# The head of a convolutional FFN: when three half-matrix sums are formed, split and queued

## The chip, the cores and the metric

One core of one Trainium2 chip runs the whole program. The metric is the device time of one launch in microseconds (us); several launches of the same program give a median. TensorE (PE) does the matrix products, VectorE (DVE) and ScalarE (ACT) the element-wise work, GpSimd (POOL) a little of it, and SyncE (SP) issues the loads and stores.

## The reference

A decoder trunk of two layers over a stream of 1024 tokens by 1024 channels, all in float32. Each layer is a mixer and then an FFN; this is the part that matters here:

```python
def conv_glu_ffn(x, w_up, conv_w, conv_b, w_down):
    h = causal_depthwise_conv(x @ w_up, conv_w, conv_b)     # w_up: 1024 x 5632, 3 taps
    gate, val = jnp.split(h, 2, axis=-1)
    return (jax.nn.silu(gate) * val) @ w_down
...
        h = h + conv_glu_ffn(rmsnorm(h, ffn_norm[layer]), ffn_up[layer], ffn_conv_w[layer],
                             ffn_conv_b[layer], ffn_down[layer])
```

## The kernel before

Channels lie on the 128 partitions and tokens along the free dimension, in halves of 512 tokens. Every float32 operand of a product is split in two: a rounded high part (ScalarE copies it, L331) and a low part, the operand less its high part (VectorE, L332; `split`, L330). A product then is three matmuls per 128 channels: high by high, high by low, low by high. So each operand costs one ScalarE and one VectorE instruction before TensorE can use it.

An FFN layer (`ffn`, L526) goes over `f` = 0 to 21. A step `f` makes 128 gate channels `g` and 128 value channels `v` for all tokens. Step 0 is a plain projection (`proj_two`, L350; 96 matmuls of 128x512). After its first four input chunks it calls the hook `norms[1].rest` (L321), which finishes the norm of the second half of the tokens: eight chunks, each a scaling on VectorE (L317), a high copy on ScalarE and a low subtraction, on VectorE for even chunks and on GpSimd for odd ones (L319).

From step 1 on, the four half products of `g` and `v` are made out of seven products instead of eight, with sums of halves of the input and of the weights (a Strassen form). With y11, y21, y12, y22 the four quarters of the normed input `hT` (channels 0 to 511 or 512 to 1023 of the first or second 512 tokens), the input sums are T1 = y12 - y11, T2 = y22 - T1, T3 = y22 - y12 and T4 = y21 - T2. `tokens` (L624) forms them in place in `hT` and splits them: T1 into the second half of `AH`/`AL`, T2, T3, T4 into `TH`/`TL`. The products of a step stand in the loop of L661 in this order, 12 matmuls of 128x512 each: `11` and `21` (with weights `a`), `2` (`b`), `1` (`d`), `3` (`c`), `22` (`b`), `4` (`c`), into the PSUM tiles `X` and `YZ`. The weights of step `f` + 1 are prepared during step `f` by `prep_a` (the split of the gate weights), `prep_s` (sums), `prep_b`, `prep_c` and `prep_d` (splits); each frees a load buffer `wst`, and the load of the next weights waits for that. The `Tail` of a step (convolution taps at L607, silu, product, store) runs during the next step. The tail of step 0 reads its `g` and `v` straight out of PSUM (`0g`, `0v`), where two tiles of this size fit.

A scheduler puts the instructions of each engine in one order, which the engine keeps: an instruction that waits holds all behind it on its engine. So the place of an instruction in its engine's order says what it waits behind.

There are two FFN layers, so the head of the FFN comes twice, at about 355 to 417 us and 1519 to 1578 us of the span. The hook `norms[1].rest` is also called at the head of the odd layer's mixer, at about 1040 to 1060 us.

Of the kernel before, what the change touches and what calls it, by code (L numbers as in the profile page):

```python
# [24 lines left out]
NF = DFF // P  # L25
# [110 lines left out]
def trunk(ctx: ExitStack, tc: tile.TileContext, x, mix0_norm, mix0_w_in, lru_conv_w, lru_conv_b,  # L136
# [149 lines left out]
    class Norm:  # L286
# [24 lines left out]
            dve.scalar_tensor_tensor(r0, q, 1.5, r0, op0=ALU.add, op1=ALU.mult)  # L311
            self.r = r0

        def chunk(self, c):
            s = HALF[self.h]
            y = self.hT[:, c, s] if self.put else t2(f"y_{self.name}{c}")
            dve.scalar_tensor_tensor(y, self.hT[:, c, s], self.gcol(c), self.r,  # L317
                                     op0=ALU.mult, op1=ALU.mult)
            split(AH[:, c, s], AL[:, c, s], y, pool if c % 2 else dve)  # L319

        def rest(self):  # L321
            self.rstd()
            for c in range(DC):
                self.chunk(c)

    def rsqrt_set():

        act.activation(junk, eps, AF.Abs_reciprocal_sqrt)

    def split(h, l, src, eng=None):  # L330
        act.copy(h, src)  # L331
        (eng or dve).tensor_tensor(l, src, h.bitcast(F32), op=ALU.subtract)  # L332

    def proj_half(ps, w, s, hook=None):
        wh, wl = w
# [190 lines left out]
    def ffn(ly, norms):  # L526
# [39 lines left out]
        def prep_b(f):  # L566
            w = ws[f]
            w["b"] = W.pair()
            split(*w["b"], w["g"])
            W.done()  # L570
# [50 lines left out]
                dve.tensor_tensor(self.cv, self.cv, self.cg, op=ALU.mult)  # L621
                nc.sync.dma_start(hid[ly][:, self.f], self.cv)

        def tokens():  # L624

            hT = st["hT"]
            y11, y21, y12, y22 = (hT[:, a, s] for s in HALF for a in (slice(0, 4), slice(4, 8)))
            for k in (slice(0, 2), slice(2, 4)):
                dve.tensor_tensor(y11[:, k], y12[:, k], y11[:, k], op=ALU.subtract)  # L629
                dve.tensor_tensor(y12[:, k], y22[:, k], y12[:, k], op=ALU.subtract)  # L630
                dve.tensor_tensor(y22[:, k], y22[:, k], y11[:, k], op=ALU.subtract)
                split(TH[:, 0, k], TL[:, 0, k], y22[:, k])
            split(*Y["1"], y11)
            split(*Y["3"], y12)
            dve.tensor_tensor(y21, y21, y22, op=ALU.subtract)  # L635
            split(*Y["4"], y21)


        prev = Tail(0, *proj_two(f"{ly}g0", f"{ly}v0", norms[1].rest))
        prep_a(1)  # L640
        prep_s(1, 0)
        prep_s(1, 1)
        tokens()
        prep_b(1)
        prep_d(1)
        prep_c(1)
        prev.ident()
        close_h()
        w2_cm = tc.tile_pool(name=f"w2{ly}", bufs=1)
        W.more = w2[0] = w2_cm.__enter__()  # L650
        slots = [(AH[:, c], AL[:, c]) for c in range(DC)]
        th6, tl6 = (t.rearrange("p a b t -> p (a b t)").rearrange("p (s t) -> p s t", t=T)
                    for t in (TH, TL))
# [5 lines left out]
            split(*slots[slot], r)  # L659

        for f in range(1, NF):  # L661
            w, nxt = ws.pop(f), f + 1 if f + 1 < NF else None
# [11 lines left out]
            prev.silu()  # L674
            dve.tensor_tensor(g[:, HALF[0]], y_, p1, op=ALU.add)
            prev.conv_v(1)
            prod(X, w["b"], 0, "2", False)
            u2 = t2(f"u2{ly}{f}")
            act.copy(u2, X)
            prev.conv_v(0)  # L680
            prev.end()
            prod(z_, w["d"], 0, "1")
            p5 = t2(f"p5{ly}{f}")
            act.copy(p5, z_)
            if nxt:
# [20 lines left out]
            prev.ident()  # L706
        W.ahead(2)
        for c in range(4, 8):
            stage(c, c)
        prev.conv_g()  # L710
        prev.silu()
        prev.conv_v(1)
        prev.conv_v(0)
        prev.end()
        W.more = w2[0] = None
        w2_cm.__exit__(None, None, None)
        fd_cm.__exit__(None, None, None)
# [663 lines left out]
```

## Time and profile before

| what | us |
|---|---|
| median of 3 runs | 2218.29 |
| lowest and highest of them | 2216.78, 2218.61 |
| the profiled execution, its own time | 2214.68 |
| its span in the trace | 2212.9 |
| TensorE busy | 2146.9 (97%) |
| VectorE busy | 1456.2 (66%) |
| ScalarE busy | 1011.1 (46%) |
| GpSimd busy | 114.3 (5%) |

Busy shares are means over a program whose stages differ. TensorE idles 66 us in all of the span; a wait in a stage where TensorE is the busiest engine lengthens the program, if nothing later takes the time up again. The views used below are the sums by stretch (windows), the waits of an engine, and the timeline of an engine, all of the one profiled execution.

### The profile page before, as it was taken

Reading aid. Unit: us, or ns where it says so; the run is one execution under the profiler, and the core shown is the slowest. Engines: PE = TensorE matmul, PEld = TensorE weight load, DVE = VectorE, ACT = ScalarE, POOL = GpSimd, SP = SyncE. Lnnn points to the kernel's source line nnn. Section 1 sums busy time; section 2 is a strip of 40 time slices with the busy share of each in tenths; the row PEclk is TensorE's granted clock in tenths of the full one; section 3 lists DMA queues with packets and bytes.
Section 4 is the critical chain, followed back from the end, with each engine's and each line's share of the span. In section 5 each row is a group of like instructions: output and inputs, shape, how many; then the busy total and the mean of one; then the engine's idle time right before and its main releaser. Section 6 shows DMA issues by size and latency. Waiting matters only on the chain. (4 is left out here: it accounts for less than half of the span.)

```text
span 2212.9 us, 25475 instructions
## 1 busy us (share of the span) xinstructions
PE 2146.9 (97%) x9789; PEld 1757.7 (79%) x9789; DVE 1456.2 (66%) x2046; ACT 1011.1 (46%) x1389; POOL 114.3 (5%) x141
## 2 busy tenths in 40 slices
PE   7999999899999999999899999899899999999998
PEld 6888887788888888887678887687688888888887
DVE  7555658977777773347476667768987777773344
ACT  6333544455555551124466575644555555551113
POOL 1000001000000000004211111001000000000000
PEclk9999999899999999999999999999999999999999
DMA  5111442222222272234222211552222222282212
GB/s 160 38 48 48 126 136 72 92 80 86 86 86 86 86 275 80 83 124 124 62 61 57 80 54 50 166 167 76 93 79 86 86 86 86 86 285 84 74 53 76
DMA packets 264353, 213.76 MB, mean 97 GB/s; under 512 B 8464, under 2 KB 233680, under 8 KB 264232
## 3 DMA queue, kind: packets, MB, share of 16 engines
q1 hardware_dynamic: 264040, 211.85, 30.8%
q8 instruction: 77, 1.26, 0.2%
q0 software_dynamic: 192, 0.30, 0.1%
q14 instruction: 44, 0.36, 0.1%
HBM read 165.94 MB, written 44.07 MB: 95 GB/s over the span
## 5 line engine op out<-in xcount | busy, mean ns | idle before, releaser
L108 ACT CAST wh<-wst 128x1024 fp32r<-128x1024 f32 (+2 forms) x134 | 134.1, 1001 | 514.9 <-PE dp L731 284.3
L109 DVE TENSOR_TENSOR wl<-wst,wh 128x1024 fp32r<-128x1024 f32 (+2 forms) x126 | 146.4, 1162 | 102.1 <-ACT wh L108 101.9
L733 DVE TENSOR_TENSOR hT_f<-dp,hT_f 128x512 f32<-128x512 f32 x96 | 65.9, 690 | 223.5 <-PE dp L731 221.9
L731 PE MATMUL dp<-AH,wh 128*128 128x512 f32 x432 | 168.1, 391 | 0.3 <-DVE hT_f L733 0.3
L731 PE MATMUL dp<-AH,wl 128*128 128x512 f32 x432 | 168.0, 389 | 0.0
L731 PE MATMUL dp<-AL,wh 128*128 128x512 f32 x432 | 167.9, 390 | 0.0
L587 PE MATMUL X<-TH,wl 128*128 128x512 f32 x312 | 124.1, 398 | 8.9 <-DVE wl L332 8.9
L587 PE MATMUL X<-TH,wh 128*128 128x512 f32 x312 | 123.9, 397 | 6.3 <-ACT p L669 5.7
L587 PE MATMUL X<-TL,wh 128*128 128x512 f32 x312 | 123.6, 396 | 0.0
L331 ACT CAST wh<-wst 128x1024 fp32r<-128x1024 f32 x78 | 80.9, 1054 | 64.5 <-PE YZ L587 45.8
L607 DVE SCALAR_TENSOR_TENSOR cg<-g,par_c,cg 128x1023 f32<-128x1023 f32 x84 | 107.5, 1280 | 1.8 <-ACT cg L601 1.6
L607 DVE SCALAR_TENSOR_TENSOR cv<-v,par_c,cv 128x1023 f32<-128x1023 f32 x84 | 107.2, 1276 | 0.1
L338 PE MATMUL op<-AH,wh 128*128 128x512 f32 x256 | 101.9, 398 | 1.9 <-DVE yt L1191 1.3
L338 PE MATMUL op<-AH,wl 128*128 128x512 f32 x256 | 100.5, 392 | 0.0
L338 PE MATMUL op<-AL,wh 128*128 128x512 f32 x256 | 100.4, 392 | 0.0
L332 DVE TENSOR_TENSOR wl<-wst,wh 128x1024 fp32r<-128x1024 f32 x78 | 95.2, 1222 | 7.2 <-ACT wh L331 7.1
L731 PEld LDWEIGHTS dp<-AH,wh 128*128 128x128 f32 x432 | 81.1, 188 | 18.4 <-DVE hT_f L733 0.7
L731 PEld LDWEIGHTS dp<-AL,wh 128*128 128x128 f32 x432 | 81.1, 188 | 17.5 <-DVE AL L332 0.4
L731 PEld LDWEIGHTS dp<-AH,wl 128*128 128x128 f32 x432 | 81.1, 188 | 16.9
L587 PE MATMUL YZ<-AH,wh 128*128 128x512 f32 x208 | 81.2, 390 | 0.0
L587 PE MATMUL YZ<-AL,wh 128*128 128x512 f32 x208 | 81.0, 389 | 0.0
L587 PE MATMUL YZ<-AH,wl 128*128 128x512 f32 x208 | 80.9, 389 | 0.0
(424 smaller groups left out, 5762.3 us busy)
## 6 DMA issues: line engine op xcount, KB each, us to landing
wst<-in_ffn_up_dram SPq DMA_DIRECT2D x88, 512.0 KB
hid<-cv SPq DMA_DIRECT2D x44, 512.0 KB
hr<-hid SPq DMA_DIRECT2D x44, 512.0 KB
wst<-in_mix_w_in_dram SPq DMA_DIRECT2D x40, 512.0 KB
wst<-in_ffn_down_dram SPq DMA_DIRECT2D x35, 512.0 KB
wst<-in_mix_w_out_dram SPq DMA_DIRECT2D x32, 512.0 KB
hdr<-hT_o SPq DMA_DIRECT2D x32, 256.0 KB
hT_f<-hdr SPq DMA_DIRECT2D x16, 512.0 KB
```

The costliest lines, as they stand in the source:

```text
L108: self.nc.scalar.copy(wh[:, :k, :m], w[:, :k, :m])
L109: (eng or self.eng).tensor_tensor(wl[:, :k, :m], w[:, :k, :m], wh[:, :k, :m].bitcast(F32), op=ALU.subtract)
L331: act.copy(h, src)
L332: (eng or dve).tensor_tensor(l, src, h.bitcast(F32), op=ALU.subtract)
L338: pe.matmul(ps, a[:, k], b[:, k, s], start=(k == 0 and i == 0), stop=(k == DC - 1 and i == 2))
L587: pe.matmul(ps, a[:, k0 + k], b[:, k], start=(first and k == 0 and i == 0), stop=(k == 3 and i == 2), skip_group_check=True)
L607: dve.scalar_tensor_tensor(dst[:, dl:], src[:, :T - dl], taps[j](c), dst[:, dl:], op0=ALU.mult, op1=ALU.add)
L731: pe.matmul(ps, p_[:, k], q_[:, s], start=(k == 0 and i == 0), stop=(k == n - 1 and i == 2))
L733: dve.tensor_tensor(hT[:, oc, s], ps, hT[:, oc, s], op=ALU.add)
```

## The change

`norms[1].rest` puts all eight low subtractions on VectorE. This holds for both FFN heads and for the mixer's head.

In the FFN head, `tokens` is taken apart. T1 and T2 come first, T1 in place by one instruction and T2 in two halves into scratch tiles of its own (two of the ring `t4`); T2 is split at once, then come the weights `b` and `d` of step 1. The result of step 0 is copied out of PSUM into two `t4` tiles, so its tail reads SBUF. What is left of `tokens` is called in step 1 behind ScalarE's copy `p1` of the first product: T1's split and half of T3 stand behind T2's splits, the rest of T3, the weights `c`, T4 and the copy of `0v` stand behind `p1` in ScalarE's order and behind T1's split in VectorE's (`tc.issue_after` adds an order on the same engine, and no wait across engines). T3 and T4 are split in halves. The whole tail of step 0 goes to the end of step 1. A small edit leaves the list of weights in place (`ws[f]` for `ws.pop(f)`).

```diff
-    def chunk(self, c):
+    def chunk(self, c, eng=None):
...
-            split(AH[:, c, s], AL[:, c, s], y, pool if c % 2 else dve)
+            split(AH[:, c, s], AL[:, c, s], y, eng or (pool if c % 2 else dve))
     def rest(self):
         self.rstd()
         for c in range(DC):
-            self.chunk(c)
+            self.chunk(c, dve)
...
-        def tokens():
-            hT = st["hT"]
-            y11, y21, y12, y22 = (hT[:, a, s] for s in HALF for a in (slice(0, 4), slice(4, 8)))
-            for k in (slice(0, 2), slice(2, 4)):
-                dve.tensor_tensor(y11[:, k], y12[:, k], y11[:, k], op=ALU.subtract)
-                dve.tensor_tensor(y12[:, k], y22[:, k], y12[:, k], op=ALU.subtract)
-                dve.tensor_tensor(y22[:, k], y22[:, k], y11[:, k], op=ALU.subtract)
-                split(TH[:, 0, k], TL[:, 0, k], y22[:, k])
-            split(*Y["1"], y11)
-            split(*Y["3"], y12)
-            dve.tensor_tensor(y21, y21, y22, op=ALU.subtract)
-            split(*Y["4"], y21)
-        prev = Tail(0, *proj_two(f"{ly}g0", f"{ly}v0", norms[1].rest))
+        p0 = proj_two(f"{ly}g0", f"{ly}v0", norms[1].rest)
         prep_a(1)
         prep_s(1, 0)
         prep_s(1, 1)
-        tokens()
+        y11, y21, y12, y22 = (st["hT"][:, a, s] for s in HALF
+                              for a in (slice(0, 4), slice(4, 8)))
+        tt2 = [t4(f"T2{i}{ly}").rearrange("p (k t) -> p k t", k=2) for i in range(2)]
+        ks = slice(0, 2), slice(2, 4)
+        dve.tensor_tensor(y11, y12, y11, op=ALU.subtract)
+        for k, t in zip(ks, tt2):
+            dve.tensor_tensor(t, y22[:, k], y11[:, k], op=ALU.subtract)
+            t2h, t2l = split(TH[:, 0, k], TL[:, 0, k], t)
         prep_b(1)
+        first = [t4(f"{n}0{ly}") for n in "gv"]
+        act.copy(first[0], p0[0])
         prep_d(1)
-        prep_c(1)
-        prev.ident()
-        close_h()
...
+        def tokens(p1):
+            with tc.issue_after(t2h.ins), tc.issue_after(t2l.ins):
+                _, t1l = split(*Y["1"], y11)
+                dve.tensor_tensor(y12[:, ks[0]], y22[:, ks[0]], y12[:, ks[0]], op=ALU.subtract)
+            with tc.issue_after(p1.ins), tc.issue_after(t1l.ins):
+                dve.tensor_tensor(y12[:, ks[1]], y22[:, ks[1]], y12[:, ks[1]], op=ALU.subtract)
+                split(TH[:, 1, ks[0]], TL[:, 1, ks[0]], y12[:, ks[0]])
+                prep_c(1)
+                split(TH[:, 1, ks[1]], TL[:, 1, ks[1]], y12[:, ks[1]])
+                act.copy(first[1], p0[1])
+                for k, t in zip(ks, tt2):
+                    dve.tensor_tensor(y21[:, k], y21[:, k], t, op=ALU.subtract)
+                    split(TH[:, 2, k], TL[:, 2, k], y21[:, k])
+            close_h()
...
+        prev = Tail(0, *first)
...
             prod(X, w["a"], 0, "11")
             p1 = t2(f"p1{ly}{f}")
-            act.copy(p1, X)
+            late = f == 1
+            c1 = act.copy(p1, X)
+            if late:
+                w2_cm = tokens(c1)
...
-            prev.conv_g()
+            if not late:
+                prev.conv_g()
...
             if nxt:
                 prep_c(nxt)
+            if late:
+                prev.whole()
             prev = Tail(f, g, v)
             prev.ident()
```

In the rows of the orders below the number behind a name tells buffers apart, and lines from L331 down to L332 keep their numbers in both kernels.

**The end of the norm on VectorE, first FFN head.** `hT_o` <- `r_no` is the scaling of a chunk, `AL` its low subtraction, `wst` the last weight sum of step 1. Before:

```order
L317 SCALAR_TENSOR_TENSOR hT_o_1722<-hT_o_1722,par_a,r_no_2497 128x512 x3
L332 TENSOR_TENSOR AL<-hT_o_1722,AH 128x512
L317 SCALAR_TENSOR_TENSOR hT_o_1722<-hT_o_1722,par_a,r_no_2497 128x512
L332 TENSOR_TENSOR AL<-hT_o_1722,AH 128x512
L317 SCALAR_TENSOR_TENSOR hT_o_1722<-hT_o_1722,par_a,r_no_2497 128x512 x3
L332 TENSOR_TENSOR AL<-hT_o_1722,AH 128x512
L317 SCALAR_TENSOR_TENSOR hT_o_1722<-hT_o_1722,par_a,r_no_2497 128x512
L332 TENSOR_TENSOR AL<-hT_o_1722,AH 128x512
```

Now:

```order
L317 SCALAR_TENSOR_TENSOR hT_o_1722<-hT_o_1722,par_a,r_no_2497 128x512 x3
L332 TENSOR_TENSOR AL<-hT_o_1722,AH 128x512 x3
L317 SCALAR_TENSOR_TENSOR hT_o_1722<-hT_o_1722,par_a,r_no_2497 128x512 x3
L332 TENSOR_TENSOR AL<-hT_o_1722,AH 128x512 x3
L317 SCALAR_TENSOR_TENSOR hT_o_1722<-hT_o_1722,par_a,r_no_2497 128x512 x2
L564 TENSOR_TENSOR wst_2395<-wst_2395 128x512
L332 TENSOR_TENSOR AL<-hT_o_1722,AH 128x512 x2
```

The four subtractions of the odd chunks, which stood on GpSimd, have joined the four of the even ones here.

**The sums and splits on VectorE, right behind.** L629 to L635 (now L645 to L666) are the sums, `TL` the low parts of T2, T3, T4, `AL` of 128x4x512 that of T1, `wl` and `dl` those of the weights of step 1 (`wst_2395`: `b`; `wst_2434`: `c`). Before:

```order
L564 TENSOR_TENSOR wst_2395<-wst_2395 128x512
L629 TENSOR_TENSOR hT_o_1722<-hT_o_1722 128x2x512 x2
L630 TENSOR_TENSOR hT_o_1722<-hT_o_1722 128x2x512 x2
L631 TENSOR_TENSOR hT_o_1722<-hT_o_1722 128x2x512 x2
L332 TENSOR_TENSOR AL<-hT_o_1722,AH 128x4x512
L332 TENSOR_TENSOR TL_2477<-hT_o_1722,TH_2476 128x1024 x2
L332 TENSOR_TENSOR TL_2477<-hT_o_1722,TH_2476 128x2048
L635 TENSOR_TENSOR hT_o_1722<-hT_o_1722 128x4x512
L332 TENSOR_TENSOR wl_2638<-wst_2395,wh_2637 128x1024
L332 TENSOR_TENSOR dl_2644<-s_2615,dh_2643 128x512
L332 TENSOR_TENSOR wl_2648<-wst_2434,wh_2647 128x1024
L332 TENSOR_TENSOR TL_2477<-hT_o_1722,TH_2476 128x2048
```

Now:

```order
L645 TENSOR_TENSOR hT_o_1722<-hT_o_1722 128x4x512
L332 TENSOR_TENSOR wl_2630<-wst_2395,wh_2629 128x1024
L647 TENSOR_TENSOR T_2620<-hT_o_1722 128x1024
L647 TENSOR_TENSOR T_2621<-hT_o_1722 128x1024
L332 TENSOR_TENSOR dl_2639<-s_2615,dh_2638 128x512
L332 TENSOR_TENSOR TL_2477<-T_2620,TH_2476 128x1024
L332 TENSOR_TENSOR TL_2477<-T_2621,TH_2476 128x1024
L658 TENSOR_TENSOR hT_o_1722<-hT_o_1722 128x2x512
L332 TENSOR_TENSOR AL<-hT_o_1722,AH 128x4x512
L660 TENSOR_TENSOR hT_o_1722<-hT_o_1722 128x2x512
L332 TENSOR_TENSOR TL_2477<-hT_o_1722,TH_2476 128x1024
L332 TENSOR_TENSOR wl_2667<-wst_2434,wh_2666 128x1024
```

The low part of the weights `b` (`wl_2638`) stood behind eleven sums and splits and now (`wl_2630`) stands behind one sum; T2 (`T_2620`, `T_2621`) is split next, and T1, T3 and the weights `c` (`wl_2667`) follow. Behind the last row stand now: the second half of T3's split, the two sums of T4, the low part of step 2's weights `a` (`wl_2688`), T4's two splits, and only then `g` of step 1.

**The copies on ScalarE in the same stretch.** `wh` are high parts of weights, `p` the copy of the first product, `cg` and `cv` the start of step 0's tail. Before:

```order
L331 CAST wh_2637<-wst_2395 128x1024
L601 ACTIVATE cg_2653<-0g_2481,par_c_1730 128x1024
L331 CAST AH<-hT_o_1722 128x4x512
L331 CAST TH_2476<-hT_o_1722 128x2048
L331 CAST TH_2476<-hT_o_1722 128x1024 x2
L331 CAST wh_2647<-wst_2434 128x1024
L602 ACTIVATE cv_2654<-0v_2482,par_c_1730 128x1024
L669 COPY p_2677<-X_2661 128x512
L331 CAST TH_2476<-hT_o_1722 128x2048
```

Now:

```order
L331 CAST wh_2629<-wst_2395 128x1024
L651 COPY g_2635<-0g_2481 128x1024
L331 CAST TH_2476<-T_2620 128x1024
L331 CAST TH_2476<-T_2621 128x1024
L693 COPY p_2658<-X_2642 128x512
L331 CAST AH<-hT_o_1722 128x4x512
L331 CAST wh_2666<-wst_2434 128x1024
L331 CAST TH_2476<-hT_o_1722 128x1024
L664 COPY v_2636<-0v_2482 128x1024
L331 CAST wh_2687<-wst_2633 128x1024
L331 CAST TH_2476<-hT_o_1722 128x1024
L708 COPY u_2716<-X_2642 128x512
```

The copy `p` (now L693) has moved from behind T1, T2, T3 and the weights `c` to right behind T2; `0g` and `0v` are copied instead of read by the tail. TensorE's order moves with it: the product `21` of step 1 (into `YZ`) stood behind `2` and `3` in the first head, and now stands right behind `11`, ahead of `2`; in the first head four matmuls of step 2's weights `a` now stand between `2` and `3`.

## Rows read from the trace of the kernel before

**Rows 1.** Windows: start:end, length, busy per engine (instructions), granted clock, DMA.

```profile
381.70:417.33 35.63, 26.93 (x98) 20.21 (x96) 32.85 (x29) 18.80 (x20) 0.00 (x0) 0.81 0.26 80
1545.52:1578.40 32.88, 25.10 (x97) 19.25 (x96) 31.09 (x28) 16.41 (x18) 0.00 (x0) 0.84 0.26 80
354.69:381.70 27.01, 24.42 (x99) 17.86 (x98) 24.60 (x28) 12.52 (x16) 6.62 (x4) 1.00 0.03 11
1518.51:1545.52 27.01, 24.44 (x100) 17.86 (x98) 24.60 (x28) 12.52 (x16) 6.63 (x4) 1.00 0.03 11
420.00:780.00 360.00, 360.00 (x1590) 298.16 (x1590) 278.17 (x304) 188.49 (x228) 0.00 (x0) 1.00 0.28 85
```

**Rows 2.** Waits of TensorE, first FFN head: waiter <- releaser: us, times, longest.

```profile
PE X L587 <- DVE wl L332: 4.4, 1, 4.4
PE X L587 <- ACT p L669: 2.8, 1, 2.8
PE 0g L338 <- POOL AL L332: 1.8, 3, 0.8
PE 0g L338 <- DVE AL L332: 0.8, 2, 0.6
PE YZ L587 <- DVE g L675: 0.8, 1, 0.8
PE X L587 <- ACT u L679: 0.7, 1, 0.7
```

**Rows 3.** Timeline: start, length, engine, line, work; TensorE after the second wait.

```profile
393.26 0.63 PE L587 MATMUL X<-TH,wh 128*128 128x512 f32 x1
393.68 0.63 PE L587 MATMUL X<-TL,wh 128*128 128x512 f32 x1
```

**Rows 4.** Timeline, VectorE, first FFN head (merged rows: first start to last end).

```profile
363.24 2.07 DVE L317 SCALAR_TENSOR_TENSOR hT_o<-hT_o,par_a,r_no 128x512 f32<-128x512 f32 x3
365.23 0.68 DVE L332 TENSOR_TENSOR AL<-hT_o,AH 128x512 fp32r<-128x512 f32 x1
365.83 1.77 DVE L317 SCALAR_TENSOR_TENSOR hT_o<-hT_o,par_a,r_no 128x512 f32<-128x512 f32 x1
...
377.98 2.35 DVE L630 TENSOR_TENSOR hT_o<-hT_o 128x1024 f32<-128x1024 f32 x2
380.25 2.35 DVE L631 TENSOR_TENSOR hT_o<-hT_o 128x1024 f32<-128x1024 f32 x2
382.52 2.28 DVE L332 TENSOR_TENSOR AL<-hT_o,AH 128x2048 fp32r<-128x2048 f32 x1
384.73 4.55 DVE L332 TENSOR_TENSOR TL<-hT_o,TH 128x1024 fp32r<-128x1024 f32 x3
...
391.40 1.21 DVE L332 TENSOR_TENSOR wl<-wst,wh 128x1024 fp32r<-128x1024 f32 x1
...
396.48 1.27 DVE L607 SCALAR_TENSOR_TENSOR cg<-0g,par_c,cg 128x1023 f32<-128x1023 f32 x1
```

**Rows 5.** Timeline, GpSimd, the same head.

```profile
365.38 1.67 POOL L332 TENSOR_TENSOR AL<-hT_o,AH 128x512 fp32r<-128x512 f32 x1 [28.06 <-ACT AH L331]
```

**Rows 6.** Waits of TensorE, second FFN head (the row on p is as above).

```profile
PE X L587 <- DVE wl L332: 4.5, 1, 4.5
...
PE X L587 <- ACT wh2x L331: 0.4, 1, 0.4
```

**Rows 7.** Timeline, TensorE, head of the odd layer's mixer.

```profile
1060.12 0.60 PE L996 MATMUL 1q<-AH,wh 128*128 128x512 f32 x1 [3.85 <-DVE qs L1065]
```

**Rows 8.** Windows, the same place.

```profile
1060.31:1063.72 3.41, 3.41 (x9) 2.66 (x9) 0.92 (x2) 1.26 (x3) 0.76 (x2) 0.50 0.37 82
```

**Rows 9.** Timeline, SyncE's queue and ScalarE: a weight load and who waits for it.

```profile
407.27 8.43 SPq L87 DMA_DIRECT2D wst<-in_ffn_up_dram  x2
...
410.90 1.05 ACT L331 CAST wh2x<-wst 128x1024 fp32r<-128x1024 f32 x1 [0.29 <-DMA wst<-in_ffn_up_dram]
```

More of the change, by code (lines that the diff above doesn't have):

```diff
@@ L330, in split @@
     def split(h, l, src, eng=None):
-        act.copy(h, src)
-        (eng or dve).tensor_tensor(l, src, h.bitcast(F32), op=ALU.subtract)
+        return (act.copy(h, src),
+                (eng or dve).tensor_tensor(l, src, h.bitcast(F32), op=ALU.subtract))
     def proj_half(ps, w, s, hook=None):
@@ L622, in end, with rest, whole @@
                 nc.sync.dma_start(hid[ly][:, self.f], self.cv)
-        def tokens():
-            hT = st["hT"]
-            y11, y21, y12, y22 = (hT[:, a, s] for s in HALF for a in (slice(0, 4), slice(4, 8)))
-            for k in (slice(0, 2), slice(2, 4)):
-                dve.tensor_tensor(y11[:, k], y12[:, k], y11[:, k], op=ALU.subtract)
-                dve.tensor_tensor(y12[:, k], y22[:, k], y12[:, k], op=ALU.subtract)
-                dve.tensor_tensor(y22[:, k], y22[:, k], y11[:, k], op=ALU.subtract)
-                split(TH[:, 0, k], TL[:, 0, k], y22[:, k])
-            split(*Y["1"], y11)
-            split(*Y["3"], y12)
-            dve.tensor_tensor(y21, y21, y22, op=ALU.subtract)
-            split(*Y["4"], y21)
-        prev = Tail(0, *proj_two(f"{ly}g0", f"{ly}v0", norms[1].rest))
+            def rest(self):
+                self.conv_g()
+                self.silu()
+                self.conv_v(1)
+                self.conv_v(0)
+                self.end()
+            def whole(self):
+                self.ident()
+                self.rest()
+        p0 = proj_two(f"{ly}g0", f"{ly}v0", norms[1].rest)
         prep_a(1)
@@ L642, in ffn @@
         prep_s(1, 1)
-        tokens()
+        y11, y21, y12, y22 = (st["hT"][:, a, s] for s in HALF
[6 more added lines that the diff above has]
+            t2h, t2l = split(TH[:, 0, k], TL[:, 0, k], t)
         prep_b(1)
+        first = [t4(f"{n}0{ly}") for n in "gv"]
+        act.copy(first[0], p0[0])
         prep_d(1)
-        prep_c(1)
-        prev.ident()
-        close_h()
-        w2_cm = tc.tile_pool(name=f"w2{ly}", bufs=1)
-        W.more = w2[0] = w2_cm.__enter__()
+        def tokens(p1):
[12 more added lines that the diff above has]
+            close_h()
+            w2_cm = tc.tile_pool(name=f"w2{ly}", bufs=1)
+            W.more = w2[0] = w2_cm.__enter__()
+            return w2_cm
+        prev = Tail(0, *first)
         slots = [(AH[:, c], AL[:, c]) for c in range(DC)]
@@ L661, in ffn @@
         for f in range(1, NF):
-            w, nxt = ws.pop(f), f + 1 if f + 1 < NF else None
+            w, nxt = ws[f], f + 1 if f + 1 < NF else None
             X = psml(f"X{ly}{f}")
@@ L668, in ffn @@
             p1 = t2(f"p1{ly}{f}")
-            act.copy(p1, X)
+            late = f == 1
+            c1 = act.copy(p1, X)
+            if late:
+                w2_cm = tokens(c1)
             if nxt:
                 prep_a(nxt)
-            prev.conv_g()
+            if not late:
+                prev.conv_g()
             prod(y_, w["a"], 4, "21")
-            prev.silu()
+            if not late:
+                prev.silu()
             dve.tensor_tensor(g[:, HALF[0]], y_, p1, op=ALU.add)
-            prev.conv_v(1)
+            if not late:
+                prev.conv_v(1)
             prod(X, w["b"], 0, "2", False)
@@ L679, in ffn @@
             act.copy(u2, X)
-            prev.conv_v(0)
-            prev.end()
+            if not late:
+                prev.conv_v(0)
+                prev.end()
             prod(z_, w["d"], 0, "1")
@@ L709, in ffn @@
             stage(c, c)
[L710 to L714, printed above, removed]
+        prev.rest()
         W.more = w2[0] = None
```

## The prediction

> **What bounds the kernel now.** First read the windows [rows 1]. The last row is the bulk of an FFN: 360 us in which TensorE never idles, 1590 matmuls, 0.2264 us each (0.2267 with the few missing records), a product of 12 in 2.72 us. There nothing is to be had from the order of the other engines. The first two rows are the stretches this change is about: from the first product of step 1 to the first matmul of product `21` of step 2, each with exactly 96 matmuls of the same size. At the full pace they take 96 x 0.2267 = 21.8 us; they took 35.6 and 32.9. The excess is 13.9 us in the first FFN and 11.1 us in the second. The next two rows are the norms ahead of them, also 96 big matmuls each plus two small float32 ones of some 1.1 us together: 27.0 us each, 4.1 more than 22.9.
>
> Second, the waits say what ends this idle time [rows 2, 6]. In the first stretch TensorE waits 2.8 us until its own bank `X` is copied (ACT `p`), 4.4 us for the low part of the weights `b` (DVE `wl`), and twice 0.7 to 0.8; in the second 4.5 and 0.4, and the same 2.8 for `p`. In the norm it waits five times for the low part of a chunk, 2.6 us in all, 1.8 of it for GpSimd; the second norm repeats this (its busy time is the same to 0.02 us [rows 1]).
>
> Third, the clock. In the first stretch the granted clock is 0.81 in the mean [rows 1]: after the two long waits matmuls start 0.42 to 0.43 us apart, the pace of the 1.2 GHz level [rows 3]. A mean of 0.81 over 35.6 us is 35.6 x 0.19 / 0.5 = 13.5 us at that level; in the second stretch 32.9 x 0.16 / 0.5 = 10.5 us. So the 13.9 us are 8.7 us of waits, 0.1 us of slower first matmul behind each, and the rest, near 4.8 us, the low clock.
>
> Fourth, VectorE. It is busy 32.9 of 35.6 us there and 24.6 of 27.0 in the norm [rows 1], and the wait of 4.4 us ends with the row at 391.40, `wl` [rows 4]: eleven sums and splits for products 1, 2, 3 and 4 stood ahead of it. So it is a matter of order on VectorE.
>
> **The change, part by part.** Start-to-start costs on VectorE come from [rows 4]: 0.67 us for a scaling (three from 363.24 to 365.23), 0.60 for a 512 subtraction (365.23 to 365.83), 1.14 for a 1024 one (377.98 to 380.25 for two), 2.21 for a 2048 one (382.52 to 384.73).
>
> *Norm.* Four low subtractions go from GpSimd to VectorE. The row at 365.83 is a scaling that took 1.77 us where its kind takes 0.74 (2.07 for three that overlap); it lies under GpSimd's 1.67 us subtraction of 365.38 to 367.05 [rows 5]. So each of the four GpSimd rows holds up a VectorE row by about 1.0 us, and a subtraction on VectorE costs 0.60: 4 x 0.60 - 4 x 1.0 = 1.6 us less on VectorE, not 2.4 more. The Trainium skill, Perfetto Trace Analysis (Optimizing Scalar/DVE Operations), says that a saturated VectorE may gain from work given to another engine, "or even GPSIMD", with the warning that the two share a read port. By its first half this edit would cost 2.4 us a norm; the row above is on the side of the warning.
>
> Walk VectorE's new order from 363.24, where nothing ahead has changed: 3 scalings to 365.2, 3 subtractions to 367.0, 3 and 3 again to 370.8, 2 scalings and a weight sum to 372.8, the last 2 subtractions to 374.0. The last low part is there at 374.0, where GpSimd's was at 375.9 (the last of the five waits). The chunks come in threes, which leaves about one wait of 0.2 us by the same walk. TensorE starts step 1 some 2.9 us earlier (2.6 of waits and 5 x 0.1, less that one): at 378.8 instead of 381.7.
>
> *Sums.* Walk on: T1 (one row of 2.21) to 376.2, `wl` of `b` to 377.3, T2 to 379.6, `dl` to 380.2, T2's low parts to 382.5, half of T3 to 383.6, T1's low part to 385.8, half of T3 to 387.0, its low part to 388.1, `wl` of `c` to 389.2, the other low part to 390.4, T4 to 392.7, `wl` of step 2's `a` to 393.8, T4's low parts to 396.1, then `g`. ScalarE's copies keep ahead: it was busy 18.8 of 35.6 us [rows 1], and the added copies of `0g` and `0v` are two instructions of 128x1024, about 1.1 us each by the cast at 410.90 [rows 9]. Queuing behind `p` holds nothing up that VectorE could have taken: `p` ends near 382, when VectorE is still at T2.
>
> TensorE: product `11` from 378.8, `21` from 381.5, `2` from 384.2. What `2` needs is there at 382.6 (T2) and 378.5 (`wl`): the waits of 2.8 and 4.4 us are gone, partly since `21` now stands ahead of `2` as 2.72 us of cover, partly since `wl` comes 14 us sooner. `2` ends at 386.9. Then four matmuls of step 2, 0.9 us, and product `3`, which needs `wl` of `c` (done 389.3) and the second half of T3 (done 390.5): waits of about 1.6 and 0.2 us. `3` ends at 391.9, and the next matmul wants `wl` of step 2's `a`, done at 393.9: 2.0 us. That is what is late next, and I find nothing later that is. The waits come to 3.8 us and 0.4 us of slow first matmuls, against 13.9: **9.7 us** there, with 2.9 in the norm **12.6 us** in the first head. It rests on the clock staying at 2.4 GHz: the longest wait is 2.0 us instead of 4.4.
>
> The load for step 2 waits for `wl` of `b`. It is issued near 378.5, 14 us sooner; a load takes 3.6 us from issue (407.27) to the cast that waits (410.90) [rows 9], so step 2's first weights are there at 382, before ScalarE comes to them. On SyncE only the store of step 0 moves, behind two loads; it is read back only after the last step.
>
> *Second head.* The same walk, but there step 2's matmuls don't stand between `2` and `3` or behind `3`: `3` waits 2.5 and 0.2 us, and product `1` comes at once behind it, into the tile that `g` of step 1 still reads. `g` stands behind T4's sums there (done 393.4), `3` ends at 392: 1.5 us. With 0.5 us for step 2's load (0.4 now [rows 6]) that is 4.7 us and 0.5 for first matmuls, against 11.1: **5.9 us**, with the norm **8.8 us**.
>
> *Mixer's head.* The same hook. TensorE waits 3.85 us for VectorE, which reads `1q` out of PSUM behind the norm [rows 7], and its next 3.41 us run at the 1.2 GHz level [rows 8]: nine matmuls where 15 would fit, 1.4 us. By the costs above VectorE is through 1.6 us sooner. So 1.6 us of the wait, and, if the shorter one lets the clock stand, 1.4 more: between 1.6 and 3.0, I take **2.6**, nearer the upper end, since 2.6 us of waits in a norm left the granted clock at 1.00 [rows 1, 2].
>
> *What is put off.* Step 0's tail: four taps of 1.19 and a product of 1.14 us, from 396.48 on [rows 4], 5.9 us of VectorE, go to step 2. In the bulk VectorE is busy 278.2 of 360.0 us [rows 1], 14.7 of 19.0 us a step: 4.3 us free each. So the backlog is gone within two steps; up to then step 1's and 2's tails are late, and nothing waits for those but the stores. I take 0.3 us for it; its upper bound is all of it, 5.9 us a head.
>
> Sum: 12.6 + 8.8 + 2.6 - 0.3 = 23.7 us. The profiled execution took 2214.68 us, 1.8 us around its span; less 23.7 that is 2191.0. It lies 3.6 us under the median of the runs, 2218.29; against that the forecast is **2194.6 us**, 1.1% faster.
>
> **The rivals.** (a) *The backlog is not free.* If step 0's tail delays the reads of `X` and `YZ`, TensorE waits for PSUM in steps 2 and 3: at most 5.9 us a head, 11.8 in all, and 2206. For: VectorE is busy 92% of the head [rows 1]. Against: the free 4.3 us a step.
>
> (b) *VectorE is the bound, and order changes nothing.* Then only its work counts: 1.6 us less in three norms, 5 us, 2213. Against: it does the work of the tail in the head today, which is put off, and TensorE waited for rows that stand early now.
>
> (c) *The clock falls all the same.* The new waits are short but lie within 8 us. If each head has its 13.5 us at the low level as now, half of it is lost, 6.8 us, less what the waits cover: at most 13.5 us in two heads, 2208. The Trainium skill, TensorE: Matmul & The Clock Gate (A second HAM failure mode: psum-queue depth-cycling), tells of a kernel whose short pauses between groups of matmuls made the clock go to and fro and cost throughput. Here the norm has five waits, up to 0.8 us each, at a granted clock of 1.00 [rows 1, 2], which speaks against it.
>
> (d) *Slower.* The same mechanism, all through: were both stretches of 96 matmuls to run at 1.2 GHz, they would take 21.8 us more each, 43.5, and the time would be 2218.3 - 23.7 + 43.5 = 2238. It decides from 23.7 / 0.2267 = 105 of the 192 matmuls at the low level. Today a wait of 4.4 us brings no more than 13.5 us.
>
> (e) *The change doesn't do what it says*: T2's scratch comes out of the ring `t4` of four, which `g` and `v` of steps 1 and 2 need too. Were `g` of step 1 to wait for T4 (the scratch's last reader), VectorE would hold `1` up in both heads by T4's two splits, 2.3 us each: 2199, within the forecast's range.
>
> **How the numbers follow.** Forecast, with (e): 0.72, 2188 to 2201. (a) 0.13, (c) 0.08, (b) 0.04, (d) 0.03. The low end of the range is 2188: the waits of the walk gone as well, 3.8 + 4.7 us less, with 2 us back for the runs' spread. The high end is 2208, which takes in (a) and (c). Runs of this kernel tell 0.2% (4.4 us) from no change: 2213.9 and 2222.7 are the bounds. Forecast, (a) and (c) lie below: 0.93. Of (b) all lies about the bound: 0.04 for no change. Slower 0.03.
>
> **What would show it.** Right: no GpSimd rows in the norm's second half, scalings of 0.74 us; TensorE's wait for `p` gone, the wait for `wl` of 2 us behind product `3` in the first head and for `g` before product `1` in the second; granted clock 1.00 in both heads; 96 matmuls in 26 us (first) and 27 us (second); the wait at the mixer's head about 2 us. Wrong: waits in steps 2 to 4 for ACT copies of `X` or VectorE's `g` (a), a granted clock under 0.95 in a head (c, d), or VectorE rows that take longer than those of now.

## The result, and the profile after

The changed kernel takes 2193.31 us in the median of its runs (2192.57 to 2196.03) against 2217.86 before (four runs; the 2218.29 of the table ahead is the median of three of them): a ratio of 0.9892, 95% interval 0.9875 to 0.9909. Two more sets of runs of the same kernel gave 2192.55 (0.9887, 0.9871 to 0.9904) and 2193.93 (0.9898, 0.9882 to 0.9915). The forecast was 2194.6.

The profiled execution of the first set took 2196.03 us with a span of 2194.3, the longest of its four; those of the other two have spans of 2190.5 and 2190.6. Below, **after** is the first and **after3** the last of them, and both are read, since they differ in one thing that matters.

The windows of after, in the columns of [rows 1]: the norm, the 96 matmuls behind it (up to the start of the 97th), and the same two of the second head. The count of a row takes in matmuls that only touch the window's ends:

```profile
355.14:378.30 23.16, 23.13 (x100) 18.14 (x98) 20.75 (x29) 9.86 (x14) 0.00 (x0) 1.00 0.04 13
378.30:406.03 27.73, 24.50 (x97) 18.78 (x96) 26.15 (x27) 19.38 (x21) 0.00 (x0) 0.94 0.26 76
1507.94:1531.10 23.16, 23.15 (x99) 18.15 (x98) 20.75 (x29) 9.86 (x14) 0.00 (x0) 1.00 0.03 12
1531.10:1558.26 27.16, 24.67 (x98) 18.86 (x97) 27.09 (x28) 18.45 (x20) 0.00 (x0) 0.94 0.21 61
```

And of after3, the 96 matmuls behind the first norm and those behind the second:

```profile
377.79:404.00 26.21, 22.98 (x97) 17.57 (x96) 26.05 (x27) 18.93 (x20) 0.00 (x0) 1.00 0.23 65
1527.31:1554.46 27.15, 23.21 (x97) 17.73 (x96) 27.08 (x28) 18.45 (x20) 0.00 (x0) 1.00 0.21 61
```

The norm took 27.01 us in [rows 1] and takes 23.16 now, GpSimd has no row in it, and VectorE is busy 20.75 us there instead of 24.60, in a window that is shorter by as much. The 96 matmuls behind the first norm took 35.63 us; they take 26.21 in after3, at a granted clock of 1.00, and 27.73 in after, at 0.94. Those behind the second took 32.88 and take 27.16 and 27.15.

The waits of TensorE in the first head (after), then those of the second head (after3), in the columns of [rows 2]:

```profile
PE X L587 <- DVE wl L332: 2.0, 1, 2.0
PE X L587 <- ACT wh L331: 0.8, 1, 0.8
PE X L587 <- ACT u L708: 0.4, 1, 0.4
```

```profile
PE YZ L587 <- DVE g L703: 1.4, 1, 1.4
PE X L587 <- DVE TL L332: 0.8, 1, 0.8
PE X L587 <- ACT u L708: 0.7, 1, 0.7
PE X L587 <- DVE wl L332: 0.6, 1, 0.6
PE X L587 <- ACT wh2x L331: 0.4, 1, 0.4
```

All waits of the norm, the 2.8 us for `p` and the 4.4 for `wl` of [rows 2] are gone. What is left is 3.2 us in the first head (after) and 3.9 in the second (after3).

VectorE's timeline of the first head in after, which answers [rows 4]:

```profile
367.48 2.07 DVE L317 SCALAR_TENSOR_TENSOR hT_o<-hT_o,par_a,r_no 128x512 f32<-128x512 f32 x3
...
374.40 2.28 DVE L645 TENSOR_TENSOR hT_o<-hT_o 128x2048 f32<-128x2048 f32 x1
376.61 1.22 DVE L332 TENSOR_TENSOR wl<-wst,wh 128x1024 fp32r<-128x1024 f32 x1
...
390.76 2.35 DVE L666 TENSOR_TENSOR hT_o<-hT_o,T 128x1024 f32<-128x1024 f32 x2
393.03 1.22 DVE L332 TENSOR_TENSOR wl<-wst,wh 128x1024 fp32r<-128x1024 f32 x1
394.17 2.35 DVE L332 TENSOR_TENSOR TL<-hT_o,TH 128x1024 fp32r<-128x1024 f32 x2
```

Three scalings take 2.07 us, where one that lay under a GpSimd row took 1.77 [rows 4, 5]. The `wl` of product `2` starts at 376.61 instead of 391.40. The last `wl`, that of step 2's weights, ends at 394.25 and ends the wait of 2.0 us.

The time by stage, from the starts of the first matmuls of each stage in the timelines, as changes against the kernel before (us). Its stages: norm and bulk of the first FFN, from the `0g` matmul that opens the norm (354.69) to the down product `dp` (795.41); from there to the odd mixer's `1q` (1038.10); the mixer's head, to `1g` (1088.43); the rest of the mixer, to the norm's sum `ms_no` (1479.52); the second FFN head and all behind it. What lies ahead of the first stage moves by -0.1 to +0.7 in these executions.

| kernel | first FFN | to the mixer | mixer's head | rest of it | second FFN to end |
|---|---|---|---|---|---|
| after | -11.56 | +1.29 | -3.95 | +3.21 | -8.07 |
| after2 | -11.56 | 0.00 | -4.01 | +1.67 | -8.45 |
| after3 | -13.04 | +0.36 | -4.00 | +2.37 | -7.94 |
| hook_only | -3.45 | -0.22 | -3.98 | +1.31 | -1.50 |
| sums_only | -11.30 | -0.15 | +0.74 | +1.05 | -5.11 |
| ffn_hook | -11.49 | +0.74 | -0.04 | +1.13 | -8.06 |
| tail_early | -9.37 | +1.14 | -4.00 | +2.00 | -6.31 |
| t1_twice | -9.04 | +0.60 | -3.97 | +0.12 | -4.40 |
| no_order | -13.13 | -0.12 | -3.94 | +3.11 | -6.65 |
| a2_first | -14.21 | +0.55 | -3.95 | +3.08 | -11.04 |
| a2_again | -14.17 | +0.96 | -3.98 | +1.06 | -11.70 |

### The profile page after: what moved, and what is told of

Same layout as the page of the kernel before. It is cut to its first block, busy times and chain, and to the rows that moved or that the text cites. A ratio compares the mean times of both kernels' runs of the same rounds, so it can differ in the third digit from the quotient of the medians.

```text
span 2194.3 us, 25469 instructions
## 1 busy us (share of the span) xinstructions
PE 2145.4 (98%) x9789; PEld 1758.5 (80%) x9789; DVE 1451.8 (66%) x2062; ACT 1016.1 (46%) x1397; POOL 95.0 (4%) x129
## 4 chain that ended last, share of the span: by engine, by line
PE 84%; DVE 8%; issue 3%; DMA 2%; ACT 2%; POOL 1%; SPq 0%; DVEq 0%; ACTq 0%; POOLq 0%
PE dp L759 19%; PE X L587 18%; PE YZ L587 14%; PE op L338 8%; PE 0cp L338 2%; PE f L794 2%; PE 0vb L338 2%; PE 0bp L338 2%; PE 1q L1024 2%; PE 0xa L338 2%; PE 0ga L338 2%; PE 1u L1024 2%; PE 1v L1024 1%; PE acc L1190 1%; DMA hr<-hid 1%
## 5 line engine op out<-in xcount | busy, mean ns | idle before, releaser
L607 DVE SCALAR_TENSOR_TENSOR cg<-g,par_c,cg 128x1023 f32<-128x1023 f32 x88 | 112.7, 1280 | 3.0 <-ACT cg L601 2.9
L607 DVE SCALAR_TENSOR_TENSOR cv<-v,par_c,cv 128x1023 f32<-128x1023 f32 x88 | 112.4, 1277 | 0.1
L331 ACT CAST wh<-wst 128x1024 fp32r<-128x1024 f32 x78 | 80.7, 1054 | 55.8 <-PE YZ L587 36.4
L332 DVE TENSOR_TENSOR wl<-wst,wh 128x1024 fp32r<-128x1024 f32 x78 | 94.9, 1221 | 5.7 <-ACT wh L331 5.7
```

The lines of the kernel that those rows point to most:

```text
L331: return (act.copy(h, src), (eng or dve).tensor_tensor(l, src, h.bitcast(F32), op=ALU.subtract))
L607: dve.scalar_tensor_tensor(dst[:, dl:], src[:, :T - dl], taps[j](c), dst[:, dl:], op0=ALU.mult, op1=ALU.add)
```

## The experiments

### Each half of the change alone: hook_only, sums_only

The kernel before with the hook alone:

```diff
-                self.chunk(c)
+                self.chunk(c, dve)
```

> The kernel before with one edit: the norm's hook puts all eight low subtractions on VectorE; sums, splits and tail stay as they were. Theory of the prediction (the terms add): 2.9 us in each FFN head and 2.6 in the mixer's head, 8.4 in all, so 2217.9 - 8.4 = 2209.5; the waits for ACT `p` (2.8) and DVE `wl` (4.4) behind the norm stay as long as they were. Rival 1 (VectorE sets the end of the head, so a norm that TensorE leaves earlier only waits longer later): what VectorE saves counts alone, 1.6 us in each of three norms, 2213, and the two waits together grow by about 1.3 us in each head. Rival 2 (the subtractions cost VectorE 0.60 each and free nothing): 2.4 us more in each norm, 2225.

Measured: 2207.09 us against 2216.44, ratio 0.9955 (0.9941 to 0.9970), 9.35 us faster. The waits of TensorE in its first FFN head:

```profile
PE X L587 <- DVE wl L332: 4.6, 1, 4.6
PE X L587 <- ACT p L669: 4.4, 1, 4.4
```

The sum is about what the added terms gave (8.4), but it is made up otherwise. In the mixer's head it is 4.0 us and not 2.6. In the FFN heads TensorE reaches step 1 sooner, and 1.5 us of that go into a longer wait for `p` (4.4 for 2.8 in [rows 2]), as rival 1 said: the second FFN gains 1.5 us, not 2.9. The first gains 3.45, with 10.24 us of low clock where there were 13.65. So rival 1 has the mechanism in the FFN heads, and the mixer makes up for it in the sum.

The kernel after with the hook as it was:

```diff
-                self.chunk(c, dve)
+                self.chunk(c)
```

> The kernel after with one edit: the hook's odd chunks go back to GpSimd; the new order of sums, splits and tail stays. Theory of the prediction: the order alone is worth 9.7 and 5.9 us less 0.3, so 2217.9 - 15.3 = 2202.6; three waits for POOL `AL` come back in each norm, and the mixer's head waits 3.9 us again at a granted clock near 0.5 behind it. Rival 1 (order and hook each need the other, since VectorE sets the head): less than 10 us of the 24.5 are left, 2208 or more. Rival 2 (the hook adds nothing once the order is right): 2193 to 2196.

Measured: 2200.72 against 2216.44, ratio 0.9929 (0.9914 to 0.9944), 15.7 us faster, where the forecast had 15.3. The waits of TensorE in its first head:

```profile
PE X L587 <- DVE wl L332: 1.9, 1, 1.9
PE 0g L338 <- POOL AL L332: 1.8, 3, 0.8
PE 0g L338 <- DVE AL L332: 0.8, 2, 0.6
```

The norm has its five waits back and the mixer's head its wait, while the 2.8 and the 4.4 us stay away: rivals 1 and 2 fall. 9.35 and 15.7 add up to 25.1 us, against 23.1 to 25.5 for both together in three sets of runs. In the first head it looks otherwise (-3.45 and -11.30, but -11.56 to -13.04 for both); there sums_only ran at a clock of 1.00 throughout and after did not. Against after3, which had 1.00 there too, 3.45 + 11.30 is 1.7 us too much. That is half of the 3.41 us of low clock that hook_only has less than the kernel before, a gain that sums_only makes as well.

### The mixer's head alone: ffn_hook

```diff
-                self.chunk(c, dve)
+                self.chunk(c, dve if self.put else None)
```

> The kernel after with one edit: in the mixer's head alone the hook's odd chunks stay on GpSimd. Theory of the prediction: the term of the mixer's head comes back, 1.6 to 3.0 us, taken as 2.6, with a wait of 3.9 us for VectorE and 3.41 us at the low level behind it: 2195 to 2196.5, and both FFN heads as in the kernel after. Rival (the run with the whole hook on GpSimd lost 7.4 us, so the hook is worth most of that in the mixer): 2198 or more.

Measured: 2198.28 us, ratio 0.9914 (0.9899 to 0.9928), against 2192.55 for after2: 5.7 us, so the rival's number came. By stage the mixer's head takes 4.0 us longer than in after, which is more than the theory's 3.0 and less than the 5.7. The FFN stages stay within 0.1 us of after, and the rest of the mixer takes 2.1 us less, where after has 3.41 us more at the low level. What makes up the 5.7 us besides the 4.0 stays open. Three views say where the 4.0 us are. VectorE in the mixer's norm, before:

```profile
1049.76 0.75 DVE L317 SCALAR_TENSOR_TENSOR y_nf<-hT_f,par_a,r_nf 128x512 f32<-128x512 f32 x1 [1.18 <-POOL AL L332]
...
1055.93 0.75 DVE L317 SCALAR_TENSOR_TENSOR y_nf<-hT_f,par_a,r_nf 128x512 f32<-128x512 f32 x1 [1.18 <-POOL AL L332]
...
1059.28 0.69 DVE L1065 SCALAR_TENSOR_TENSOR qs<-1q,qs 64x512 fp32r<-64x512 f32 x1
```

and in after, with TensorE's first matmuls behind the wait:

```profile
1047.93 0.69 DVE L1093 SCALAR_TENSOR_TENSOR qs<-1q,qs 64x512 fp32r<-64x512 f32 x1
```

```profile
1047.70 0.50 PE L1156 MATMUL S<-kh,qs 128*128 128x128 f32 x2 [1.25 <-POOL kh L1101]
1048.03 0.39 PE L1024 MATMUL 1q<-AH,wh 128*128 128x512 f32 x1
```

Here VectorE itself stood still for GpSimd, twice for 1.18 us. Against the stage's start (1038.10 and 1028.28) its second `qs` comes 1.53 us sooner, which is the 1.6 of the prediction. The wait shrinks by more, 3.85 [rows 7] to 1.25, since two `S` matmuls stand at its end now and `1q` goes on before the second `qs` is done. That is 2.6 us. The 3.41 us at 0.50 behind the wait [rows 8] are gone too (1.4 us by the prediction's own count): together the 4.0.

### The tail that is put off: tail_early

```diff
-            if not late:
-                prev.conv_g()
+            prev.conv_g()
...
-            if late:
-                prev.whole()
```

(and so for the other parts of the tail).

> The kernel after with one edit: step 0's tail goes back to its places within step 1 (it still reads the copies in SBUF). Theory of the prediction: putting it off costs nothing later, and where it stands now 5.9 us of VectorE work lie ahead of `g` and of the sums of step 2; with the 4.3 us that VectorE has free in a step most of it is covered, so 1 to 3 us are lost in each head, 2195 to 2199, with new waits in steps 1 and 2 for VectorE's `g` or for copies out of `YZ`. Rival (a) of the prediction (the backlog of a tail that is put off delays steps 2 and 3): the kernel becomes faster, by up to 5.9 us a head, below 2193 and down to 2181.

Measured: 2197.32, ratio 0.9912 (0.9897 to 0.9927), 3.4 to 4.8 us slower than the three sets of after; by stage 2.2 us in the first head (against after, with the same stretch of low clock) and 1.6 to 2.1 in the second. The waits of its second head:

```profile
PE X L587 <- ACT wh2x L331: 2.6, 1, 2.6
PE YZ L587 <- DVE g L702: 1.4, 1, 1.4
```

The wait for step 2's `wh2x` is 2.6 us instead of 0.4. So putting the tail off is worth about 2 us a head, and rival (a) as this run had it, a faster kernel, is refuted.

### What the wait left over is worth: t1_twice

T1's low part is made twice, ahead of T4:

```diff
                 act.copy(first[1], p0[1])
+                dve.tensor_tensor(Y["1"][1], y11, Y["1"][0], op=ALU.subtract)
```

> The kernel after with one more instruction in each head: T1's low part, 2.21 us of VectorE, is made a second time with the same values, ahead of T4. Theory 1 (VectorE's order sets the end of the head, and the wait is what is left over): the wait for `wl` in the first head grows from 2.0 to 4.2 us, in the second head that for `g` appears with about 2.2 us; 4.4 us for both heads, and, if a wait of 4.2 us brings the 10 us and more of low clock that one of 4.4 us brought in the kernel before, another 3 to 5 us: 2198 to 2203. Theory 2 (other engines end the head, VectorE has that room): no change, 2192 to 2196.

Measured: 2199.74, ratio 0.9919 (0.9904 to 0.9933), 7.2 us over after2. TensorE's longest waits in its first and its second head:

```profile
PE X L587 <- DVE wl L332: 4.2, 1, 4.2
...
PE YZ L587 <- DVE g L704: 3.6, 1, 3.6
```

Both grew by 2.2 us, the whole of the added instruction: VectorE's order sets the end of both heads. By stage it is 2.5 us (against after) and 3.5 to 4.0. The clock did not answer as expected in the first head: behind a wait of 4.2 us there are 3.41 us at the low level, as behind 2.0 us in after, where the kernel before had 13.65 in its head with 4.4 and 2.8 us of waits. In the second head 6.83 us at the low level (from 1546.58) go with the wait of 3.6 us, where after2 and after3 have none with one of 1.4, and this head loses more than the 2.2 us.

### The added orders: no_order

```diff
-            with tc.issue_after(t2h.ins), tc.issue_after(t2l.ins):
+            if True:
...
-            with tc.issue_after(p1.ins), tc.issue_after(t1l.ins):
+            if True:
```

> The kernel after without the two added orders (behind T2's splits; behind the copy of the first product on ScalarE and T1's split on VectorE); the code stands in the same order. Theory of the prediction (what counts is VectorE's order, and the copy of the first product is not what TensorE waits for, since product `21` covers it): the scheduler puts sums and copies elsewhere by some instructions, waits move, and the time stays within 2 us of the kernel after, 2192 to 2196. Rival (the order behind the copy carries the gain): ScalarE's casts stand ahead of that copy, TensorE waits 2 to 3 us for it before product 2 in each head, and the low clock comes with it: 2199 or more.

Measured: 2191.91, ratio 0.9885 (0.9870 to 0.9900), against 2192.55 for after2: no difference. Waits of its first head:

```profile
PE X L587 <- DVE wl L332: 1.8, 1, 1.8
PE YZ L587 <- ACT g L651: 1.3, 1, 1.3
```

A wait of 1.3 us for the copy of `0g` takes the place of those of 0.8 and 0.4; the last wait is again that for step 2's `wl`. So the two added orders, the queue behind the first product's copy among them, bring nothing that can be measured here. VectorE's order in the first head stays as it was but for two rows that come earlier (the low parts of T1 and of the weights `c`), since the order of the program is the same. The gain lies in that order: T1, T2 and the weights `b` first, the tail last. Of its parts only the tail was run apart; what the copies of `0g` and `0v` out of PSUM bring was not measured.

### The last wait taken away: a2_first, a2_again

T4's sums and splits go behind the preparation of step 2's weights:

```diff
+                t1l = tokens(c1)
             if nxt:
                 prep_a(nxt)
+            if late:
+                w2_cm = tokens4(c1, t1l)
```

> The kernel after with one edit: the sums and splits of T4 stand behind the preparation of step 2's weights `a` in place of ahead of it. Theory 1 (the wait of 1.99 us for `wl` behind product 3 of the first head is there only because T4 stands ahead of that split, and the 3.41 us at a granted clock near 0.5 that follow it come from that wait): 2.0 us of wait and 1.6 of clock in the first head; in the second head the waits of 0.68, 0.83 and 0.63 us ahead of product 3 and behind it go as far as they come from T4, up to 2.1 us, and its 3.41 us of low clock with them, 1.6: 4 to 7 us faster, 2186 to 2189. Theory 2 (the order of VectorE only moves the wait to product 4, which needs T4): the wait stands before product 4 with about the same length and the time stays at 2192 to 2195. Theory 3 (the clock falls in each head whatever the wait): the waits go, the 3.41 us stay, 2189 to 2191.

> The same edit as in the run a2_first: T4's sums and splits behind the preparation of step 2's weights. If its 3 to 4 us are real, it lies 3 to 4 us under the kernel after in the same call, 2187 to 2191, with 0.8, 0.4 and 0.4 us of waits in each head and no stretch of low clock in either; if the difference was one between chips, it lies within 1.5 us of it.

Measured: 2188.61 (0.9874, 0.9857 to 0.9890) and 2187.58 (0.9865, 0.9850 to 0.9880), the second beside 2193.93 for after3 on the same chip. The waits of its second head (a2_again); those of the first are the same, and 0.2 more for `g`:

```profile
PE X L587 <- ACT wh L331: 0.8, 1, 0.8
PE X L587 <- ACT u L715: 0.4, 1, 0.4
PE YZ L587 <- DVE g L710: 0.4, 1, 0.4
```

The wait of 2.0 us and, in the second head, those for `TL`, `wl`, `wh2x` and 1.0 of the 1.4 for `g` are gone, and no stretch of low clock stands in either head: theory 1, with 3.9 us by the medians to after2 and 6.3 to after3. By stage the first head gains 1.2 us over after3, which had no low clock, and 2.6 over after and after2, which had it; the second gains 2.6 to 3.8. This version beats both kernels.

### The same kernel again: after2, after3

> The kernel after, unchanged, beside the next kernels and profiled once more. In its first profile each head had 3.41 us at a granted clock near 0.5 behind its waits, and the span was 2194.3 us, the longest of its four runs. Theory 1 (the fall is decided by the waits, which are the same in each execution): the two stretches of 3.41 us stand again behind the waits of 2.0 us (first head) and of 0.7, 0.8 and 0.6 us (second head). Theory 2 (it depends on how the waits lie in time, which differs from one execution to the next): the same waits, to 0.1 us, and at least one of the two stretches is gone or is another length. The time: 2192 to 2196.

> The kernel after once more, beside the kernel with step 2's weights ahead of T4 (next run) on the same chip. Theory 1 (waits are the same in each execution, the low clock behind them is not): waits of 0.8, 0.4 and 2.0 us in the first head and 0.7, 0.8, 0.6 and (if the clock stays up there) 1.4 us in the second, to 0.1 us; the stretches at a granted clock near 0.5 in the heads may be there or not, 3.41 us each. The time: 2192 to 2196. Theory 2 (the second head's fall in the first profile of this kernel was one odd execution): no such stretch in the second head, one in the first.

The same wait in three executions of one kernel, TensorE's timeline around it. After:

```profile
394.30 0.50 PE L587 MATMUL X<-AH,wl 128*128 128x512 f32 x1 [1.99 <-DVE wl L332]
...
395.66 0.63 PE L587 MATMUL X<-AL,wh 128*128 128x512 f32 x1
396.09 0.63 PE L587 MATMUL X<-AH,wl 128*128 128x512 f32 x1
```

After3:

```profile
393.81 0.50 PE L587 MATMUL X<-AH,wl 128*128 128x512 f32 x1 [1.97 <-DVE wl L332]
394.15 0.39 PE L587 MATMUL X<-AH,wh 128*128 128x512 f32 x1
394.38 0.39 PE L587 MATMUL X<-AL,wh 128*128 128x512 f32 x1
```

The waits of the first head agree to 0.1 us in all three. In after and after2 (1.95 us) matmuls start 0.43 us apart soon behind it, for 3.41 us at a granted clock of 0.50; in after3 they go on 0.23 us apart. In the second head only after has such a stretch. So theory 2: the same waits bring the fall in one execution and not in another. What decides was not found. The price is plain in the first head, 13.04 against 11.56, or 27.73 us for the 96 matmuls against 26.21: 1.5 us for one stretch. In the second head it is nothing, 27.16 us with it and 27.15 without, since there the wait for `g` comes behind it: in after that wait does not show, in the other two it takes 1.4 us.

## Why the prediction was right, point by point

**Norm.** Forecast 2.9 us each, measured 27.01 - 23.16 = 3.85 in both heads. VectorE's walk was right: T1 starts 10.72 us after the first scaling (374.40 against 363.68), forecast 10.8 (374.0 against 363.24). It is the hook that does it: in hook_only the norm takes 23.19 us. The mis-sized term is what a wait costs TensorE, "2.6 of waits and 5 x 0.1". In after3 matmuls follow at 0.227 us; across the wait of 0.79 the starts lie 386.91 - 385.73 = 1.18 apart, and the matmul behind it takes 0.34 to the next start:

```profile
385.73 0.39 PE L587 MATMUL X<-TH,wl 128*128 128x512 f32 x1
386.91 0.50 PE L587 MATMUL X<-AH,wh 128*128 128x512 f32 x1 [0.79 <-ACT wh L331]
387.25 0.40 PE L587 MATMUL X<-AL,wh 128*128 128x512 f32 x1
```

That is 1.18 + 0.34 - 2 x 0.227 = 1.07 us for a wait printed as 0.79: some 0.27 more, not 0.1; the five waits of the norm before, read in the same way, give 0.27 to 0.28 each. The idle time counts from the modelled end of the matmul ahead, 0.39 us after its start, though at full pace the next would have started 0.227 after it. With five waits, 2.6 + 5 x 0.27 = 3.95: so much of the 4.1 us that the prediction had itself counted as the norm's excess. The one wait of 0.2 us that it left standing did not come. The Trainium skill, Perfetto Trace Analysis (Optimizing Scalar/DVE Operations), holds that it may make sense to give work of a saturated VectorE away, to GpSimd too, and warns of the port that the two share; the trace is on the side of the warning, with 3.85 us less for taking four rows back.

**Sums, first head.** VectorE's walk was right, once the start is allowed for (0.44 us later in after): the last `wl` ends at 394.25, forecast 393.9; the wait behind product `3` is 2.0, forecast 2.0. The waits ahead of it are 0.8 and 0.4 for a forecast of 1.6 and 0.2, and they are other ones, both for ScalarE (`wh`, `u`) where the forecast had VectorE. The step that failed there is "ScalarE's copies keep ahead". Its timeline in after, just ahead of the wait of 0.8 us:

```profile
385.40 1.02 ACT L664 COPY v<-0v 128x1024 f32<-128x1024 f32 x1
386.31 1.05 ACT L331 CAST wh<-wst 128x1024 fp32r<-128x1024 f32 x1
```

The added copy of `0v` stands ahead of the cast of step 2's weights, and TensorE waits for that till 387.42. It cost nothing in the end, since VectorE's `wl` was later. 96 matmuls take 26.21 us in after3 where 26 was forecast. By stage the head gives 13.04 us there, and 11.56 with the stretch of low clock, for a forecast of 12.6.

**Second head.** Right: ahead of and in `3` 2.1 us of waits (three in a row, for ScalarE's `u`, then VectorE's `TL` and `wl`) for a forecast of 2.7, for `g` 1.4 for 1.5, for the load 0.4 for 0.5; 96 matmuls in 27.15 us where 27 was forecast; by stage 7.9 to 8.5 us, forecast 8.8 less 0.15. Norm and head together come to 9.6 us by the windows: 3.85 and 32.88 - 27.15 = 5.73. A part is given back four steps on, which the last point shows.

**Mixer's head.** Forecast 2.6, at most 3.0; measured 4.0 in every kernel with that hook. VectorE's 1.6 us came (1.53), and all of the low clock went; mis-sized was the wait, which shrank by 2.6, since TensorE's order behind the wait changed as well. That step read the order of VectorE alone. Behind it 1.1 to 3.2 us are lost again: these executions, t1_twice aside, have 3.41 us at 0.50 near 1100 us, which before had not. In t1_twice, without it, the loss is 0.12. sums_only and ffn_hook, whose mixer's head is that of before, have the stretch too and lose 1.05 and 1.13 us, so it does not come from the hook in the mixer. One more such stretch in the rest of the mixer (6.83 us in a row for 3.41) goes with the 3.1 to 3.2 of after, no_order and a2_first. The wait ahead of the fall near 1100 us, before and then after:

```profile
1115.30 0.51 PE L1128 MATMUL S<-kh,qs 128*128 128x512 f32 x1 [2.02 <-DVE sm L1142]
```

```profile
1101.81 0.65 PE L1156 MATMUL S<-kh,qs 128*128 128x512 f32 x1 [2.02 <-DVE sm L1170]
```

The same 2.02 us, once with a full clock behind it and once without. Why stays open; the prediction had put the mixer behind its head at nothing.

**The clock.** "Granted clock 1.00 in both heads" was wrong for after (0.94 in both), which by the prediction's own sign, under 0.95, speaks for (c); for after2 it was wrong in the first head alone, and for after3 it was right. Rival (c) held in part, at 1.5 us a stretch where it costs at all, not 6.8 a head. Of the Trainium skill's page TensorE: Matmul & The Clock Gate (A second HAM failure mode: psum-queue depth-cycling), that frequent short pauses between groups of matmuls make the clock go to and fro: the trace agrees in so far as the clock fell behind waits of 2.0 us, and shows that it need not, with the same waits at 1.00 in after3.

**The rest.** (a) fell as a rival with tail_early. There are late waits of its kind all the same: none in the steps behind the first head, but in the second FFN one for `p` near 1615 us, with one for `g`, in all three executions of the kernel after and not before. TensorE's waits there (after2), and VectorE's row of the same step that waited itself:

```profile
PE X L587 <- ACT p L693: 0.6, 1, 0.6
PE YZ L587 <- DVE g L703: 0.2, 1, 0.2
```

```profile
1607.36 0.69 DVE L560 TENSOR_TENSOR s<-wst 128x512 f32<-128x512 f32 x1 [2.00 <-DMA wst<-in_ffn_up_dram]
```

VectorE stood 2.0 us for a load of weights, its taps came late, ScalarE's silu behind them, and `p` behind that. The waits come to 0.9 + 0.2 us (after), 0.6 + 0.2 (after2) and 0.3 + 0.15 (after3); the 84 matmuls around them take 1.65, 1.33 and 1.03 us longer than before, where 0.15 a head was put in. tail_early has no wait for `p` there, but neither has a2_again, in which the tail is put off too; so it is not shown that the tail causes it. Why that load is late was not followed.

(b) fell with sums_only, (d) did not come near, and of (e) no trace shows a wait for T2's scratch. The sum of 23.7 us stands against 24.6, 25.5 and 23.1 by the medians, and 22.4, 22.3 and 18.6 by the profiles against that of before, whose own time lay 3.6 us under its median; the 18.6 is the execution with the most low clock. That the median came within 1.3 us of the forecast is in part luck: in these three executions the mixer's head gave 1.4 us more than was put in and the first head from 0.9 less to 0.6 more; the second gave 0.2 to 0.7 less, and 1.6 to 4.9 us went in stretches for which the prediction had no term. Of those, the 0 to 1.3 us between the first FFN's down product and the mixer were not followed.

## What to carry to other kernels

Where TensorE waits for VectorE at the head of a stage, walk VectorE's queue with start-to-start costs, and put first what the first products need; the row that ends last then names the next move, as T4 did here for 4 to 6 us more. Count a wait of TensorE as its printed length and some 0.27 us more, as measured here, and read the order of both engines where a wait ends. An order that is added on an engine is worth trying without.

## What the runs showed that had not been expected

- GpSimd's low parts hold VectorE up in two ways: a scaling beside them takes 1.77 us for 0.74 [rows 4, 5], and in the mixer VectorE stood still 1.18 us twice until GpSimd was done.
- One kernel with the same waits, to 0.1 us, ran with 3.41 us at a granted clock of 0.50 behind a wait of 2.0 us or with none. In t1_twice a wait of 4.2 us brought no more than that, but one of 3.6 us went with 6.83.
- A stretch of low clock ahead of a wait for another engine cost nothing (second head), one behind the last wait 1.5 us (first head).
